# A hybrid attention/SSD block on one core: products grouped by unit, decay off GpSimd, a later B-times-C step, and an output split by token tile

## The chip, the core and the metric

One NeuronCore of a Trainium2 chip runs the whole kernel. Its engines are TensorE (PE, with its weight loads shown apart as PEld), VectorE (DVE), ScalarE (ACT), GpSimd (POOL) and SyncE (SP), which issues most of the DMAs. The metric is the device time of one execution in microseconds. The time before the change is 2100.9 us, the median of three runs (2100.33 to 2101.01).

## The reference

The input is 256 tokens of width 2048, in f32. Two token mixers work on one normalised input and are merged by sigmoid gates; a gated MLP with a short convolution follows.

```python
h = rms_norm(x, norm_mix_pre)
q, k, v, z, xbc, dt, g_sb, g_ssd = split(h @ w_in)
o_sb = stick_breaking_attention(q, k, v)          # 16 heads x 128
xs, bm, cm = split(silu(causal_dwconv(xbc, ...)))  # width 4
dt = softplus(dt + dt_bias); a = -exp(a_log)
y = ssd_scan(xs, dt, a, bm, cm)                    # 64 heads x 64, 8 groups, state 128
y = rms_norm((y + xs * d_skip) * silu(z), ssd_norm)   # by group of 512
merged = sigmoid(g_sb) * (o_sb @ w_sb_proj) + sigmoid(g_ssd) * (y @ w_ssd_proj)
x = x + rms_norm(merged @ w_out, norm_mix_post)
h = rms_norm(x, norm_ffn_pre)
gate, val = split(causal_dwconv(h @ w_up, ...))    # width 3, 5632 each
x = x + rms_norm((gelu(gate) * val) @ w_down, norm_ffn_post)
```

In the scan, `decay` is exp of the differences of a running sum `cs`, and counts only where the later token is not before the earlier one.

## The kernel before

**Weights.** All weight matrices lie in one array of units of 128 x 1024 f32 (512 KB), in the order of their use. `load` brings a unit from memory on SP's queue, `prep` splits it: ACT casts the high part `whi` (fp32r, L63), DVE subtracts to get the low part `wlo` (L64). `unit()` hands out the next unit and prepares up to three units ahead; five raw and five split buffers rotate. Activations are stored split in the same way, high and low side by side, in chunks of 4 tiles (`a`, `h`, `o`, `m`, `y`, `f`).

**Two kinds of product.** A *feature product* leaves features on the partitions: the weight tile is loaded as stationary operand and the activations stream. `feat_tile` (L109) issues for each of 16 input tiles a high product of 512 columns (high weights by high and low activations, L112) and then a low product of 256 columns (low weights by high activations, L113), both into one PSUM bank. One unit serves 8 such pairs. `feat_mm` makes one output tile, `feat_mms` several at once. Features are made this way for dt, x, B and C of the SSD mixer, q and k, and both halves of the FFN: 169 output tiles, 2704 pairs. A *token product* (`tok_mm`, L136) leaves tokens on the partitions: activations are loaded, weights stream, with three products of 512 columns for each input tile and token tile (L145 to L147); the 256 tokens are two token tiles.

**Order.** PE runs its products in the order in which a scheduler places the program's instructions; where `manual_schedule` stands, the program's own order is kept for the engines named. The SSD stage is a loop over 8 groups: four x tiles, one B and one C tile (feature products), then z (token products, L432). The work of a group's scan, `ssd_work` (L323), is a generator that `pump` moves one step ahead: after every feature tile, and after every fourth input tile of a token product. Its steps are: transposes of x to `px`, with the products by dt (`xw`), by the skip factors (`xd`, in the buffer `xs`), the decay differences `mm` from the row broadcast `csb` (L338) and their masking on POOL (L339); B times C in `pcb` (L343), the exponential (L347) and their product; `po`, the part from the state of the first half (L353); the diagonal part `pd` for each token tile (L363); the norm; and the transposes `pt` to the chunk `y` (L385). `xw`, `xs`, `mm` and `csb` are slots of 8 KB a partition.

**Ends.** At the start, ten small products (L171) run while the first loads come; x is loaded in halves between halves of the first unit (L181, L182). At the end, the last 512 columns of `w_down` are made for both token tiles by turns (L706); then come the sums of squares (`add`), the product with the norm's gain (`gained`), the root (`last`, `newton`) for both tiles together, and nine outputs, each stored as soon as it is made, by turns from SP's and ACT's queues (L727).

Of the kernel before, what the change touches and what calls it, by code (L numbers as in the profile page):

```python
# [17 lines left out]
P = 128  # L18
# [11 lines left out]
C_N = KT + C_FB + 88  # L30

LNEXP = "natural_log_exp_and_others"
ACT_DVE = {mybir.EngineType.Activation, mybir.EngineType.DVE}
# [5 lines left out]
def block_kernel(ctx, tc, xT, xN, wts, vecs, rows, hvec, dskip, gain, out):  # L39
# [69 lines left out]
    def feat_tile(ps, hi, lo, c, act, k, last):  # L109

        w = slice(c * P, (c + 1) * P)
        nc.tensor.matmul(ps, hi[:, w], act[:, k % 4, :, :].rearrange("p s t -> p (s t)"), start=(k == 0), stop=last)  # L112
        nc.tensor.matmul(ps[:, :T], lo[:, w], act[:, k % 4, 0, :], start=False, stop=last, skip_group_check=True)  # L113

    def feat_mm(acts, name):
        ps = mm_bank(name)
        for k in range(KT):
            if k % 8 == 0:
                hi, lo = unit()
            feat_tile(ps, hi, lo, k % 8, acts[k // 4], k, k == KT - 1)  # L120
        return ps

    def feat_mms(acts, pss):

        for kc in range(4):
            for i, ps in enumerate(pss):
                if i % 2 == 0:
                    hi, lo = unit()
                for k in range(4):
                    feat_tile(ps, hi, lo, 4 * (i % 2) + k, acts[kc], 4 * kc + k, 4 * kc + k == KT - 1)  # L130

    def feat_sum(ps, dst):
        nc.scalar.copy(dst, ps[:, T:])
        nc.vector.tensor_tensor(dst, dst, ps[:, :T], op=ALU.add)

    def tok_mm(acts, nk, name):  # L136

        pss = [mm_bank(f"{name}_{t}") for t in range(2)]
        for k in range(nk):
            if k % 2 == 0:  # L140
                hi, lo = unit()
            w = slice(k % 2 * 512, k % 2 * 512 + 512)
            for t in range(2):
                ah, al = (acts[k // 4][:, k % 4, s, t * P:(t + 1) * P] for s in range(2))
                nc.tensor.matmul(pss[t], ah, hi[:, w], start=(k == 0), stop=False)  # L145
                nc.tensor.matmul(pss[t], ah, lo[:, w], start=False, stop=False)  # L146
                nc.tensor.matmul(pss[t], al, hi[:, w], start=False, stop=(k == nk - 1))  # L147
            if k % 4 == 3:
                pump()
        return pss  # L150
# [19 lines left out]
    for i in range(10):  # L170
        nc.tensor.matmul(wake[:, :P], ones, ones, start=True, stop=True)  # L171
# [35 lines left out]
    for t in range(2):  # L207
        nc.sync.dma_start(x_tok[t], xN[t * P:(t + 1) * P, :])


    dsk = const.tile([P, 64], F32, name="dsk")
    nc.gpsimd.dma_start(dsk, dskip.partition_broadcast(P))
# [110 lines left out]
    def ssd_work(g, xf, bf, cf, xs, csb):  # L323
        h8 = slice(8 * g, 8 * g + 8)
        sz, xd = xs[:, 0], xs[:, 1]
# [3 lines left out]
        for t in range(2):  # L329
            px = paux.tile([P, 512], F32, tag="aux", name=f"px{g}_{t}")  # L330
            for j in range(4):
                nc.tensor.transpose(px[:, j * P:(j + 1) * P], xf[j][:, t * P:(t + 1) * P], ident)
            nc.vector.tensor_tensor(v3(xw[:, t, :]), v3(px), bc_in(dt_tok[:, t, h8], 64), op=ALU.mult)
            nc.scalar.copy(xd[:, t, :], px)
            nc.gpsimd.tensor_tensor(v3(xd[:, t, :]), v3(xd[:, t, :]), bc_in(dsk[:, h8], 64), op=ALU.mult)
        nc.gpsimd.tensor_tensor(v3(xw[:, 2, :]), v3(xw[:, 0, :]), bc_in(dec0[:, h8], 64), op=ALU.mult)
        for t in range(2):
            nc.vector.tensor_tensor(mm[:, t, :, :], csb[:, :, t * P:(t + 1) * P], bc_in(cs_tok[:, t, h8], P), op=ALU.subtract)  # L338
            nc.gpsimd.affine_select(out=mm[:, t, :, :], in_=mm[:, t, :, :], pattern=[[0, 8], [1, P]], compare_op=ALU.is_ge,  # L339
                                    fill=-30000.0, base=0, channel_multiplier=-1)  # L340
# [3 lines left out]
        nc.tensor.matmul(pcb[:, 256:384], bf[:, P:T], cf[:, P:T], start=True, stop=True)  # L344
        nc.scalar.copy(xw[:, 3, 0:P], pcb[:, P:T])
        lnexp()
        nc.scalar.activation(mm, mm, AF.Exp)  # L347
        for t in range(2):
            cb = pcb[:, 256 * t:256 * t + P].unsqueeze(1).broadcast_to([P, 8, P])
            nc.vector.tensor_tensor(mm[:, t, :, :], mm[:, t, :, :], cb, op=ALU.mult)  # L350
# [7 lines left out]
        nc.gpsimd.tensor_tensor(xd[:, 1, :], xd[:, 1, :], off, op=ALU.add)  # L358
        yield
        for t in range(2):  # L360
            pd = paux.tile([P, 512], F32, tag="aux", name=f"pd{g}_{t}")
            for h in range(8):
                nc.tensor.matmul(pd[:, h * 64:h * 64 + 64], mm[:, t, h, :], xw[:, t, h * 64:h * 64 + 64], start=True, stop=True)  # L363
            nc.vector.tensor_tensor(xd[:, t, :], xd[:, t, :], pd, op=ALU.add)
            yield
# [40 lines left out]
    stats_x()  # L406
    for g in range(GROUPS):
        xf = []
# [19 lines left out]
        csb = slot(F32, [8, T], f"csb{g}")  # L428
        nc.gpsimd.dma_start(csb, cs_dram[8 * g:8 * g + 8, :].partition_broadcast(P))
        xs = slot(F32, [2, 2, 512], f"xs{g}")  # L430
        bg.append(ssd_work(g, xf, bcs[0], bcs[1], xs, csb))
# [13 lines left out]
    drain()  # L445
    work.close()
# [126 lines left out]
    class PostNorm:  # L573
# [14 lines left out]
        def last(self):  # L588
            nc.vector.scalar_tensor_tensor(self.v, self.ss[:, :, 3], 1.0 / 2048, self.v, op0=ALU.mult, op1=ALU.add)
            nc.scalar.activation(self.q, self.v, AF.Ln)  # L590
            nc.scalar.activation(self.r, self.q, AF.Exp, scale=-0.5)

        def newton(self):
            nc.vector.tensor_tensor(self.q, self.r, self.r, op=ALU.mult)
            nc.vector.scalar_tensor_tensor(self.q, self.q, -0.5, self.v, op0=ALU.mult, op1=ALU.mult)
            nc.vector.scalar_tensor_tensor(self.r, self.q, 1.5, self.r, op0=ALU.add, op1=ALU.mult)
# [106 lines left out]
    for n in range(4):  # L703
        gfo = tmp.tile([P, 512], F32, tag="gfo", name=f"gfo{n}")
        nc.gpsimd.dma_start(gfo, rows[2, blk(n)].partition_broadcast(P))
        ps = tok_mm(f_ch, FF_T, f"ps_fo{n}")  # L706
# [102 lines left out]
```

## Time and profile before

| | us |
|---|---|
| median of three runs | 2100.9 |
| the profiled execution, from outside | 2101.31 |
| its span, first to last instruction | 2099.6 |
| PE busy | 2072.1 |
| DVE busy | 1386.0 |
| ACT busy | 1156.9 |
| POOL busy | 152.3 |

The span is what the profile covers; the trace's times count from its start. The first tiles and the SSD groups fill the time to 524 us, the gate and the SSD projection follow to 788, attention with its gate to 1171, two projections and the norm to 1357, the FFN's up products to 1847, and w_down to 2087. A row of the trace's timeline has start, duration, engine, line, operation, what is written and read, and shape; in brackets stands how long the engine was idle before it and who ended that. Matmuls overlap, so the distance from start to start is what one costs.

### The profile page before, as it was taken

Reading aid. Unit: us, or ns where it says so; the run is one execution under the profiler, and the core shown is the slowest. Engines: PE = TensorE matmul, PEld = TensorE weight load, DVE = VectorE, ACT = ScalarE, POOL = GpSimd, SP = SyncE. Lnnn points to the kernel's source line nnn. Section 1 sums busy time; section 2 is a strip of 40 time slices with the busy share of each in tenths; the row PEclk is TensorE's granted clock in tenths of the full one; section 3 lists DMA queues with packets and bytes.
Section 4 is the critical chain, followed back from the end, with each engine's and each line's share of the span. In section 5 each row is a group of like instructions: output and inputs, shape, how many; then the busy total and the mean of one; then the engine's idle time right before and its main releaser. Section 6 shows DMA issues by size and latency. Waiting matters only on the chain.

```text
span 2099.6 us, 27950 instructions
## 1 busy us (share of the span) xinstructions
PE 2072.1 (99%) x10632; PEld 1760.7 (84%) x10632; DVE 1386.0 (66%) x1794; ACT 1156.9 (55%) x1542; POOL 152.3 (7%) x134
## 2 busy tenths in 40 slices
PE   9999999999999999999999999999999999999997
PEld 7788888888888888888888888788888888888886
DVE  6888877788544445555544566598878887854443
ACT  6767677667543334555556444475555555544442
POOL 0222102222000000000000021100000000000000
PEclk9999999999999999999999999999999999999999
DMA  8564565555555555555555746475555555565653
GB/s 297 194 205 160 190 205 186 176 199 179 187 197 192 192 194 186 180 171 171 170 172 185 274 161 210 141 250 191 189 190 190 189 189 190 191 232 202 195 193 109
DMA packets 109094, 402.79 MB, mean 192 GB/s; under 512 B 12416, under 2 KB 12672, under 8 KB 106656
## 3 DMA queue, kind: packets, MB, share of 16 engines
q1 hardware_dynamic: 104912, 380.07, 54.1%
q0 software_dynamic: 3328, 20.02, 2.7%
q8 instruction: 83, 1.36, 0.3%
q10 hardware_dynamic: 720, 0.93, 0.1%
q14 instruction: 51, 0.42, 0.1%
HBM read 396.71 MB, written 4.26 MB: 191 GB/s over the span
## 4 chain that ended last, share of the span: by engine, by line
PE 92%; POOL 2%; DVE 2%; issue 2%; DMA 1%; ACT 1%; SPq 0%; DVEq 0%; ACTq 0%; POOLq 0%
PE ps_fv L112 8%; PE ps_fg L112 8%; PE ps_qk L112 6%; PE ps_xs L112 5%; PE ps_fo L147 4%; PE ps_fo L145 4%; PE ps_fo L146 4%; PE ps_fg L113 4%; PE ps_fv L113 4%; PE ps_qk L113 3%; PE ps_ssd L147 3%; PE ps_ssd L145 3%; PE ps_ssd L146 3%; PE ps_xs L113 2%; PE ps_bc L112 2%; PE ps_z L146 2%
## 5 line engine op out<-in xcount | busy, mean ns | idle before, releaser
L64 DVE TENSOR_TENSOR wlo<-raw,whi 128x1024 fp32r<-128x1024 f32 (+1 forms) x715 | 905.1, 1270 | 601.2 <-ACT whi L63 600.6
L63 ACT CAST whi<-raw 128x1024 fp32r<-128x1024 f32 (+1 forms) x715 | 746.2, 1051 | 793.7 <-PE ps_fo L147 128.9
L112 PE MATMUL ps_fg<-h,whi 128*128 128x512 f32 x688 | 240.7, 394 | 0.0
L112 PE MATMUL ps_fv<-h,whi 128*128 128x512 f32 x688 | 240.6, 394 | 0.0
L113 PE MATMUL ps_fg<-h,wlo 128*128 128x256 f32 x688 | 190.6, 277 | 0.0
L113 PE MATMUL ps_fv<-h,wlo 128*128 128x256 f32 x688 | 190.6, 277 | 0.0
L112 PE MATMUL ps_qk<-a,whi 128*128 128x512 f32 x512 | 181.3, 398 | 0.0
L112 PE MATMUL ps_xs<-a,whi 128*128 128x512 f32 x464 | 162.9, 396 | 0.0
L112 PEld LDWEIGHTS ps_fv<-h,whi 128*128 128x128 f32 x688 | 129.0, 188 | 30.0
L112 PEld LDWEIGHTS ps_fg<-h,whi 128*128 128x128 f32 x688 | 129.0, 188 | 30.0
L113 PE MATMUL ps_qk<-a,wlo 128*128 128x256 f32 x512 | 143.5, 280 | 0.0
L145 PE MATMUL ps_fo<-whi,f 128*128 128x512 f32 x352 | 136.9, 389 | 0.0
L147 PE MATMUL ps_fo<-whi,f 128*128 128x512 f32 x352 | 136.9, 389 | 0.0
L146 PE MATMUL ps_fo<-wlo,f 128*128 128x512 f32 x352 | 136.9, 389 | 0.0
L113 PEld LDWEIGHTS ps_fg<-h,wlo 128*128 128x128 f32 x688 | 129.2, 188 | 0.0
L113 PEld LDWEIGHTS ps_fv<-h,wlo 128*128 128x128 f32 x688 | 129.2, 188 | 0.0
L113 PE MATMUL ps_xs<-a,wlo 128*128 128x256 f32 x464 | 129.0, 278 | 0.0
L112 PEld LDWEIGHTS ps_qk<-a,whi 128*128 128x128 f32 x512 | 96.1, 188 | 22.6
L145 PE MATMUL ps_z<-whi,a 128*128 128x512 f32 x256 | 103.7, 407 | 0.0
L112 PEld LDWEIGHTS ps_xs<-a,whi 128*128 128x128 f32 x464 | 87.1, 188 | 19.6
L146 PE MATMUL ps_z<-wlo,a 128*128 128x512 f32 x256 | 100.4, 392 | 1.0 <-DVE wlo L64 1.0
L147 PE MATMUL ps_z<-whi,a 128*128 128x512 f32 x256 | 100.1, 391 | 0.0
(282 smaller groups left out, 3832.5 us busy)
## 6 DMA issues: line engine op xcount, KB each, us to landing
raw<-wts SPq DMA_DIRECT2D x713, 512.0 KB, 3.8
csb<-cs_dram POOLq DMA_DIRECT2D x8, 1024.0 KB, 8.1
xt<-xN SPq DMA_DIRECT2D x2, 1024.0 KB, 10.6
csb<-gain POOLq DMA_DIRECT2D x8, 256.0 KB, 4.1
xn<-xN POOLq DMA_DIRECT2D x2, 1024.0 KB, 7.9
x_dram<-xn POOLq DMA_DIRECT2D x2, 1024.0 KB, 9.0
xe<-x_dram POOLq DMA_DIRECT2D x2, 1024.0 KB, 10.3
x<-xT SPq DMA_DIRECT2D x3, 512.0 KB, 9.2
```

The source lines that it names most:

```text
L63: nc.scalar.copy(hi, src)
L64: nc.vector.tensor_tensor(lo, src, hi.bitcast(F32), op=ALU.subtract)
L112: nc.tensor.matmul(ps, hi[:, w], act[:, k % 4, :, :].rearrange("p s t -> p (s t)"), start=(k == 0), stop=last)
L113: nc.tensor.matmul(ps[:, :T], lo[:, w], act[:, k % 4, 0, :], start=False, stop=last, skip_group_check=True)
L145: nc.tensor.matmul(pss[t], ah, hi[:, w], start=(k == 0), stop=False)
L146: nc.tensor.matmul(pss[t], ah, lo[:, w], start=False, stop=False)
L147: nc.tensor.matmul(pss[t], al, hi[:, w], start=False, stop=(k == nk - 1))
```

## The change

- **Feature products by unit.** `feat_run` issues the high products of all 8 tiles of a unit, then all low ones. In `feat_mm` the second unit goes the other way round, low first. `feat_mms` takes two banks together.
- **SSD work.** The select on GpSimd is replaced: the difference goes through Relu with sign -1 and Exp with sign -1 on ACT (so it is never above 1), and B times C is masked with `m_le` on DVE. The scaling by `dec0` and the addition of the off-diagonal part move from POOL to DVE, and so does the product with the skip factors, read from PSUM. Multiplying the decay with B times C becomes a step of its own, so `po` comes one step later, and `pd` and `pt` too. From group 1 to the end of the gate PE keeps the program's order.
- **Skip factors** are columns of the vector load; their own DMA on POOL's queue goes.
- **Start.** Twelve instead of ten small products; the first quarter of x in one load, ahead of the first unit.
- **Tail.** For the last 512 columns the last 6 input tiles are done for token tile 0 first, then for tile 1 (`tok_mm_lag`), and everything behind runs tile by tile.

```diff
-    def feat_tile(ps, hi, lo, c, act, k, last):
-        w = slice(c * P, (c + 1) * P)
-        nc.tensor.matmul(ps, hi[:, w], act[:, k % 4, :, :].rearrange("p s t -> p (s t)"), start=(k == 0), stop=last)
-        nc.tensor.matmul(ps[:, :T], lo[:, w], act[:, k % 4, 0, :], start=False, stop=last, skip_group_check=True)
+    def feat_run(tiles, acts, hi_first):
+        for high in (hi_first, not hi_first):
+            for ps, hi, lo, k in tiles:
+                a, end = acts[k // 4][:, k % 4, :, :], k == KT - 1 and high != hi_first
+                if high:
+                    nc.tensor.matmul(ps, hi, a.rearrange("p s t -> p (s t)"), start=(k == 0), stop=end, skip_group_check=True)
+                else:
+                    nc.tensor.matmul(ps[:, :T], lo, a[:, 0, :], start=False, stop=end, skip_group_check=True)
...
     def feat_mm(acts, name):
         ps = mm_bank(name)
-        for k in range(KT):
-            if k % 8 == 0:
-                hi, lo = unit()
-            feat_tile(ps, hi, lo, k % 8, acts[k // 4], k, k == KT - 1)
+        for u in range(2):
+            feat_run(w_tiles(range(8 * u, 8 * u + 8), [ps]), acts, u == 0)
...
+    def tok_mm_lag(acts, nk, name, lag=3):
+        pss = [mm_bank(f"{name}_{t}") for t in range(2)]
+        held = []
+        for k in range(nk):
+            left = (nk - 1 - k) // 2
+            if k % 2 == 0:
+                w = unit(min(WBUFS - 2, left) if left < lag else WBUFS - 2)
+            if left < lag:
+                held.append((k, w))
+                tok_step(pss, acts, k, nk, 0, *w)
+            else:
+                for t in range(2):
+                    tok_step(pss, acts, k, nk, t, *w)
+        for k, w in held:
+            tok_step(pss, acts, k, nk, 1, *w)
+        return pss
...
-    for i in range(10):
+    for i in range(12):
...
+    nc.sync.dma_start(x_raw[0], xT[:, 0:4, :])
     for i in range(2):
-        nc.sync.dma_start(x_raw[0][:, 2 * i:2 * i + 2, :], xT[:, 2 * i:2 * i + 2, :])
         nc.sync.dma_start(raw0[:, i * 512:i * 512 + 512], wts[0][:, i * 512:i * 512 + 512])
...
             nc.vector.tensor_tensor(v3(xw[:, t, :]), v3(px), bc_in(dt_tok[:, t, h8], 64), op=ALU.mult)
-            nc.scalar.copy(xd[:, t, :], px)
-            nc.gpsimd.tensor_tensor(v3(xd[:, t, :]), v3(xd[:, t, :]), bc_in(dsk[:, h8], 64), op=ALU.mult)
-        nc.gpsimd.tensor_tensor(v3(xw[:, 2, :]), v3(xw[:, 0, :]), bc_in(dec0[:, h8], 64), op=ALU.mult)
-        for t in range(2):
-            nc.vector.tensor_tensor(mm[:, t, :, :], csb[:, :, t * P:(t + 1) * P], bc_in(cs_tok[:, t, h8], P), op=ALU.subtract)
-            nc.gpsimd.affine_select(out=mm[:, t, :, :], in_=mm[:, t, :, :], pattern=[[0, 8], [1, P]], compare_op=ALU.is_ge,
-                                    fill=-30000.0, base=0, channel_multiplier=-1)
+            nc.vector.tensor_tensor(v3(xd[:, t, :]), v3(px), bc_in(dsk[:, h8], 64), op=ALU.mult)
         yield
...
+        cbm = xw[:, 3, P:3 * P]
         nc.scalar.copy(xw[:, 3, 0:P], pcb[:, P:T])
+        for t in range(2):
+            nc.vector.tensor_tensor(cbm[:, t * P:(t + 1) * P], pcb[:, 256 * t:256 * t + P], m_le, op=ALU.mult)
         lnexp()
-        nc.scalar.activation(mm, mm, AF.Exp)
+        for t in range(2):
+            m = mm[:, t, :, :]
+            nc.vector.tensor_tensor(m, csb[:, :, t * P:(t + 1) * P], bc_in(cs_tok[:, t, h8], P), op=ALU.subtract)
+            nc.scalar.activation(m, m, AF.Relu, scale=-1.0)
+            nc.scalar.activation(m, m, AF.Exp, scale=-1.0)
+        nc.vector.tensor_tensor(v3(xw[:, 2, :]), v3(xw[:, 0, :]), bc_in(dec0[:, h8], 64), op=ALU.mult)
+        yield
...
-        nc.gpsimd.tensor_tensor(xd[:, 1, :], xd[:, 1, :], off, op=ALU.add)
+        nc.vector.tensor_tensor(xd[:, 1, :], xd[:, 1, :], off, op=ALU.add)
...
     with tc.manual_schedule(engines=ACT_DVE):
-        n3.add(3, 0, ps[0])
-        n3.add(3, 1, ps[1])
-        gained(3, 0, gfo)
-        n3.last()
-        gained(3, 1, gfo)
-        n3.newton()
-        for n in range(4):
-            for t in range(2):
+        for t in range(2):
+            w = slice(t, t + 1)
+            n3.add(3, t, ps[t])
+            gained(3, t, gfo)
+            n3.last(w)
+            n3.newton(w)
+            for n in range(4):
```

How the instructions stand on the engines shows where the steps went. First PE before, in z of group 3 (`ps_z3_0` and `ps_z3_1` are its two token tiles, the second number in a name is a buffer):

```order
L145 MATMUL ps_z3_1_2380<-whi79_2446,a2_153 128x512
L146 MATMUL ps_z3_1_2380<-wlo79_2447,a2_153 128x512
L147 MATMUL ps_z3_1_2380<-whi79_2446,a2_153 128x512
L353 MATMUL po3_2524<-xw3_2417 128x512
L145 MATMUL ps_z3_0_2379<-whi80_2464,a3_172 128x512
L146 MATMUL ps_z3_0_2379<-wlo80_2465,a3_172 128x512
L147 MATMUL ps_z3_0_2379<-whi80_2464,a3_172 128x512
```

and at the end of the same z, where the first x tile of group 4 (`ps_xs4_0`) follows:

```order
L145 MATMUL ps_z3_1_2380<-whi81_2490,a3_172 128x512
L146 MATMUL ps_z3_1_2380<-wlo81_2491,a3_172 128x512
L147 MATMUL ps_z3_1_2380<-whi81_2490,a3_172 128x512
L363 MATMUL pd3_0_2565<-xw3_2417,mm3_2418 128x64 x8
L112 MATMUL ps_xs4_0_2578<-a0_117,whi82_2508 128x512
L113 MATMUL ps_xs4_0_2578<-a0_117,wlo82_2509 128x256
```

PE now, at the end of z of group 3 and through that x tile:

```order
L148 MATMUL ps_z3_1_2372<-wlo81_2478,a3_173 128x512
L149 MATMUL ps_z3_1_2372<-whi81_2477,a3_173 128x512
L389 MATMUL po3_2549<-xw3_2409 128x512
L118 MATMUL ps_xs4_0_2557<-a0_118,whi82_2495 128x512 x4
L118 MATMUL ps_xs4_0_2557<-a1_137,whi82_2495 128x512 x4
L120 MATMUL ps_xs4_0_2557<-a0_118,wlo82_2496 128x256 x4
L120 MATMUL ps_xs4_0_2557<-a1_137,wlo82_2496 128x256 x4
L120 MATMUL ps_xs4_0_2557<-a2_154,wlo83_2516 128x256 x4
L120 MATMUL ps_xs4_0_2557<-a3_173,wlo83_2516 128x256 x4
L118 MATMUL ps_xs4_0_2557<-a2_154,whi83_2515 128x512 x4
L118 MATMUL ps_xs4_0_2557<-a3_173,whi83_2515 128x512 x4
L401 MATMUL pd3_0_2612<-xw3_2409,mm3_2410 128x64 x8
```

`po3` has moved from the middle of z to its end, and `pd3_0` from the end of z behind the first x tile; the x tile's products come as 8 high, 16 low and 8 high ones instead of by turns.

POOL before, from the row load of group 3 to that of group 4:

```order
L429 DMA csb3_2376<-cs_dram_225 128x2048
L336 TENSOR_TENSOR xw3_2417<-xw3_2417,dec0_223 128x512
L335 TENSOR_TENSOR xs3_2378<-xs3_2378,dsk_201 128x512 x2
L339 AFFINE_SELECT mm3_2418<-mm3_2418 128x1024 x2
L356 DMA csb3_2376<-gain 128x512
L358 TENSOR_TENSOR xs3_2378<-xs3_2378,csb3_2376 128x512
L429 DMA csb4_2955<-cs_dram_225 128x2048
```

and now, from group 2 to group 4:

```order
L355 DMA csb2_1793<-cs_dram_224 128x2048
L392 DMA csb2_1793<-gain 128x512
L355 DMA csb3_2369<-cs_dram_224 128x2048
L392 DMA csb3_2369<-gain 128x512
L355 DMA csb4_2945<-cs_dram_224 128x2048
```

Only the two loads of a group are left on that queue.

ACT before, from its last cast on (`n3_j` are squares, `n3_q` and `n3_r` the root):

```order
L63 CAST whi713_17594<-raw713_17592 128x1024
L571 ACTIVATE n3_j30_17648,n3_ss_16039<-ps_fo3_0_17266 128x512
L571 ACTIVATE n3_j31_17650,n3_ss_16039<-ps_fo3_1_17267 128x512
L590 ACTIVATE n3_q_16042<-n3_v_16040 128x2
L591 ACTIVATE n3_r_16041<-n3_q_16042 128x2
L727 DMA out_dram<-fo0_16037 128x512
L727 DMA out_dram<-fo1_16038 128x512
L727 DMA out_dram<-fo0_16037 128x512
L727 DMA out_dram<-fo1_16038 128x256
```

and now:

```order
L65 CAST whi713_17572<-raw713_17570 128x1024
L613 ACTIVATE n3_j30_17626,n3_ss_16017<-ps_fo3_0_17244 128x512
L633 ACTIVATE n3_q_16020<-n3_v_16018 128x1
L634 ACTIVATE n3_r_16019<-n3_q_16020 128x1
L770 DMA out_dram<-fo0_16015 128x512 x2
L613 ACTIVATE n3_j31_17643,n3_ss_16017<-ps_fo3_1_17245 128x512
L633 ACTIVATE n3_q_16020<-n3_v_16018 128x1
L634 ACTIVATE n3_r_16019<-n3_q_16020 128x1
L770 DMA out_dram<-fo1_16016 128x512
L770 DMA out_dram<-fo1_16016 128x256
```

Tile 0's root and two of its stores stand ahead of tile 1's squares (`n3_j31`) in ACT's queue now.

More of the change, by code (lines that the diff above doesn't have):

```diff
@@ L38, in block_kernel @@
 @with_exitstack
-def block_kernel(ctx, tc, xT, xN, wts, vecs, rows, hvec, dskip, gain, out):
+def block_kernel(ctx, tc, xT, xN, wts, vecs, rows, hvec, gain, out):
     nc = tc.nc
@@ L125, in feat_mms @@
         for kc in range(4):
[L126 to L130, printed above, removed]
+            for i in range(0, len(pss), 2):
+                feat_run(w_tiles(range(4 * kc, 4 * kc + 4), pss[i:i + 2]), acts, True)
     def feat_sum(ps, dst):
@@ L134, in feat_sum, with tok_step @@
         nc.vector.tensor_tensor(dst, dst, ps[:, :T], op=ALU.add)
+    def tok_step(pss, acts, k, nk, t, hi, lo):
+        w = slice(k % 2 * 512, k % 2 * 512 + 512)
+        ah, al = (acts[k // 4][:, k % 4, s, t * P:(t + 1) * P] for s in range(2))
+        nc.tensor.matmul(pss[t], ah, hi[:, w], start=(k == 0), stop=False)
+        nc.tensor.matmul(pss[t], ah, lo[:, w], start=False, stop=False)
+        nc.tensor.matmul(pss[t], al, hi[:, w], start=False, stop=(k == nk - 1))
     def tok_mm(acts, nk, name):
@@ L141, in tok_mm @@
                 hi, lo = unit()
[L142 removed]
             for t in range(2):
[L144 to L147, printed above, removed]
+                tok_step(pss, acts, k, nk, t, hi, lo)
             if k % 4 == 3:
                 pump()
+        return pss
[14 more added lines that the diff above has]
+            tok_step(pss, acts, k, nk, 1, *w)
         return pss
@@ L406, in block_kernel @@
     stats_x()
+    order = work.enter_context(ExitStack())
     for g in range(GROUPS):
+        if g == 1:
+            order.enter_context(tc.manual_schedule(engines=PE))
         xf = []
@@ L445, in block_kernel @@
     drain()
+    order.close()
     work.close()
```

51 lines of the change are left out of this document (32 added, 19 removed).

## The prediction

> **What bounds the kernel now.** I read the page's busy times first, then its chain that ended last, then who TensorE (PE) waits for, then the stretches in which one kind of product runs alone.
>
> ```profile
> span 2099.6 us, 27950 instructions
> PE 2072.1 (99%) x10632; PEld 1760.7 (84%) x10632; DVE 1386.0 (66%) x1794; ACT 1156.9 (55%) x1542; POOL 152.3 (7%) x134
> PE 92%; POOL 2%; DVE 2%; issue 2%; DMA 1%; ACT 1%; SPq 0%; DVEq 0%; ACTq 0%; POOLq 0%
> PE po L353 <- ACT xw L345: 3.7, 6, 0.7
> PE pth L385 <- DVE mog L632: 2.9, 1, 2.9
> PE ps_first L112 <- DVE a L197: 2.9, 2, 2.1
> PE po L353 <- POOL xw L336: 2.4, 1, 2.4
> ```
>
> PE is busy for 2072.1 of 2099.6 us and carries 92% of the chain. So there are only two ways to gain: PE's few waits (the last four rows: total, times, longest) with the ends of the kernel, or the pace of the products themselves. The wait rows name one thing that the change touches in the middle: the product `po` of the SSD work, 3.7 + 2.4 = 6.1 us. A busy PE is not proof of full pace, so I read that from stretches (us, then busy time and count by engine; the granted clock stands before the DMA share).
>
> ```profile
> 1400.00:1840.00 440.00, 440.00 (x2540) 384.79 (x2539) 355.34 (x558) 252.84 (x399) 0.00 (x0) 1.00 0.58 191
> 560.00:780.00 220.00, 220.00 (x972) 182.19 (x971) 102.81 (x87) 89.14 (x87) 0.00 (x0) 1.00 0.57 194
> 789.00:833.00 44.00, 44.00 (x251) 38.15 (x250) 25.09 (x31) 18.11 (x23) 0.00 (x0) 1.00 0.58 191
> ```
>
> The first is the FFN with feature products alone, a high one of 512 columns and a low one of 256 by turns: 440 us / 1270 pairs = 346.5 ns a pair. The second has token products of 512 columns alone: 220 / 972 = 226.3 ns each. The third is the attention's q and k, the same pairs as in the FFN, at 44 / 125.5 = 350.6 ns. What would they take by columns alone? At half the granted clock (a stretch quoted below) a pair's 768 columns go in 11.39 - 10.75 = 0.64 us:
>
> ```profile
> 10.75 0.63 PE L112 MATMUL ps_first<-a,whi 128*128 128x512 f32 x1
> 11.18 0.41 PE L113 MATMUL ps_first<-a,wlo 128*128 128x256 f32 x1
> 11.39 0.63 PE L112 MATMUL ps_first<-a,whi 128*128 128x512 f32 x1
> ```
>
> At full clock that is 320 ns a pair and 213.3 for 512 columns. So a token product has 226.3 - 213.3 = 13 ns on top, and an FFN pair 346.5 - 320 = 26.5, twice 13. Alternating high and low costs nothing in the FFN: the 13 ns go with each product, whatever stands beside it.
>
> **The change, part by part, against the profiled execution** (2101.3 us outside, span 2099.6; the median of the three runs, 2100.9, is 0.4 lower).
>
> *Grouped high and low products* (169 feature tiles of 16 pairs: 2704 pairs). Nothing is added or removed; only neighbours change. A high product behind a high one should take what a token product takes, 227 ns. A low one behind a low one is not in the trace in long runs; the nearest place is attention, where two products of 256 columns follow each other:
>
> ```profile
> 873.50 0.40 PE L500 MATMUL za<-sr,ntri_r 128*128 128x512 f32 x1
> 873.74 0.28 PE L501 MATMUL zb<-sr,ntri_r 128*128 128x256 f32 x1
> 873.86 0.28 PE L502 MATMUL za<-sr,nones_r 128*128 128x256 f32 x1
> 873.98 0.40 PE L500 MATMUL za<-sr,ntri_r 128*128 128x512 f32 x1
> 271.07 1.89 PE L363 MATMUL pd<-xw,mm 128*128 128x64 f32 x16
> 272.77 0.48 PE L112 MATMUL ps_xs<-a,whi 128*128 128x512 f32 x1
> ```
>
> Both start 120 ns after each other. With 227 that gives 347 a pair, as now. Bounds: the 64-column products of `pd`, each with its own weight load, come every (272.77 - 271.07) / 16 = 106 ns, so loads alone do not allow less than that: 14 ns less for a low product, -38 us in all if every low one went so fast. Above, the three of attention take 480 ns against 227 + 2 x 120 = 467 by the constant, so up to 13 ns too many; as 6.7 on each low product that is +18 us. I take 120, the row that is nearest, because it is the same width and number format.
>
> The Trainium skill ("TensorE: Matmul & The Clock Gate", Part 2, on LDWEIGHTS) puts a load of 128 columns at about 107 ns; the trace agrees with that pace (106), although it records 188 ns for a load. That speaks against the change as far as it goes: a low product of 120 leaves 13 ns for the next load, where a high one left over 100. By that page the run of low products still just fits, and the sum stays.
>
> What remains is the slower pattern of q and k. 512 pairs x (350.6 - 346.5) = 2.1 us there, and 0.9 us by my estimate in the first tiles and parts of the SSD stage (some 200 pairs with the same difference): -3.0 if all run as in the FFN. Against it stands a dearer high product behind a low one, once in 16 pairs, 169 times: by the attention rows (240 against 227) 13 ns, +1 to +2. **Together -2 us (from -38 to +18).**
>
> *SSD work.* What holds `po` back now:
>
> ```profile
> L338 DVE TENSOR_TENSOR mm<-csb,cs_tok x16: 1219/1730/2064, 80.3 to 506.8; 128x1024 f32<-128x1024 f32 x16
> 258.29 4.11 POOL L339 TENSOR_SCALAR_AFFINE_SELECT mm<-mm 128x1024 f32<-128x1024 f32 x2
> 262.43 1.92 ACT L347 ACTIVATE mm<-mm 128x2048 f32<-128x2048 f32 x1 [4.85 <-POOL mm L339]
> 264.25 0.24 ACT L345 COPY xw<-pcb 128x128 f32<-128x128 f32 x1
> 264.64 1.10 PE L353 MATMUL po<-xw 128*128 128x512 f32 x2 [0.61 <-ACT xw L345]
> ```
>
> GpSimd (POOL) selects for 4.1 us, ScalarE (ACT) waits 4.85 us for it, and the small copy that `po` needs stands behind the exponential in ACT's queue. The change takes the selects away (a Relu on ACT and a masked B times C do their work), scales with `dec0` on VectorE (DVE), and moves `po` one step of 4 k later: 24 products x 226.3 = 5.4 us. The longest of the six waits was 0.7, that of the first group 2.4, so both causes go, with room: **-6.1 us (-6.1 to 0)**. Late next on that path would be the copy behind Relu on ACT, which waits for DVE's subtraction; it now has over 5 us more.
>
> What is added has to fit beside PE:
>
> ```profile
> 253.00:316.00 63.00, 62.39 (x344) 53.45 (x343) 51.33 (x70) 44.91 (x61) 12.22 (x8) 1.00 0.57 188
> L333 DVE TENSOR_TENSOR xw<-px,dt_tok 128x512 f32<-128x512 f32 x3 | 2.0, 683 | 0.0
> ```
>
> DVE is busy 51.3 of the 63 us of a group. It gets two skip products from PSUM (683 each, as L333), the `dec0` scaling and the addition of the off-diagonal part (about as much each), and two masks of 128 columns (estimate 0.25 each): +3.2. The subtraction L338 takes 1219 at best, 1730 in the middle, while POOL works; without POOL that returns about 1.0. DVE comes to about 53.5, ACT (two copies less, a Relu about as long as the exponential's 1.92 more) stays under 47. Both stay under 63, weights are split three units ahead (3 x 8 pairs x 346.5 = 8.3 us), and PE never waits for them in these groups: 0. If that cover were gone, a late split would cost at most its own length, 1.4 us, once or twice a group; that is in the third rival. The queue of POOL now holds DMA issues alone (the row and gain loads), so nothing stands before them; the removed load of the skip factors on POOL, and the 64 more columns in the vector load on SP, move 32 KB at the start: 0.
>
> *Tail.* Today:
>
> ```profile
> 2085.81 0.39 PE L147 MATMUL ps_fo<-whi,f 128*128 128x512 f32 x1
> 2086.24 0.60 ACT L571 ACTIVATE n_j<-ps_fo 128x512 f32<-128x512 f32 x1 [11.87 <-PE ps_fo L147]
> 2086.49 0.39 PE L147 MATMUL ps_fo<-whi,f 128*128 128x512 f32 x1
> 2086.95 0.69 DVE L701 TENSOR_TENSOR fo<-ps_fo,gfo 128x512 f32<-128x512 f32 x1 [11.33 <-ACT n_j L571]
> 2087.63 0.16 DVE L589 SCALAR_TENSOR_TENSOR n_v<-n_ss,n_v 128x2 f32<-128x2 f32 x1
> 2087.83 0.20 ACT L590 ACTIVATE n_q<-n_v 128x2 f32<-128x2 f32 x1 [0.23 <-DVE n_v L589]
> 2088.89 5.52 DVE L726 SCALAR_TENSOR_TENSOR fo<-fo,n_r,xe 128x512 f32<-128x512 f32 x9
> 2089.68 4.71 ACTq L727 DMA_DIRECT2D out_dram<-fo  x4
> 2094.05 0.34 ACTq L727 DMA_DIRECT2D out_dram<-fo  x1
> ```
>
> Token tile 0 is ready 18 products, 4.1 us, before tile 1 after the change. Its last product starts at 2086.49 - 4.07 = 2082.42 instead of 2085.81, 3.4 earlier. With the rows' own distances its squares start at 2082.84, the first of its four outputs at 2085.49, and the fourth ends at 2088.15 (seven whole and two half outputs take 5.52 now, so about 0.66 and 0.45 each). But ACT issues two of tile 0's stores ahead of tile 1's squares in its queue, and the second store waits for the third output, 2087.47; with 0.34 for the issue, tile 1's squares run from about 2087.9 instead of 2086.9. From there: gain product at 2088.6, its sum of squares and root as in the rows (1.94 from gain product to first output), outputs from 2090.55, three whole and two half ones in 2.9 us: 2093.4, against 2088.89 + 5.52 = 2094.41. **-1.0 us**; without the wait behind the store it would be -2, and if the stores at the end run no sooner than now, 0.
>
> *Start.*
>
> ```profile
> 8.69:15.52 6.83, 5.57 (x17) 4.80 (x18) 5.11 (x9) 5.86 (x10) 0.00 (x0) 0.50 1.03 415
> ```
>
> PE runs at half clock from 8.69 to 15.52, after it waited for the second half of the first x load; its 5.57 busy us would have been 2.8. Two more wake products, x in one load and four high products before the next data may or may not keep the clock up. The data come at the same pace, so I take 0 (-2.8, or +1.7 if another half of such a stretch came on top). The Trainium skill (same page, Part 1) says that the gate looks at free-running windows of 3.4 us and releases after a busy one: the 6.83 us are two such windows. By it, a fuller second window would give the 2.8 back.
>
> Sum: -2 - 6.1 - 1.0 + 0 = -9.1, from 2101.3 to 2092.2; less the 0.4 by which the median lies below the profiled run: **2091.8 us**.
>
> **Rivals.**
> 1. *Slower: the run of low products is paced by weight loads.* Each low product leaves PE only 120 ns to take in the next weights, sixteen times in a row, where now a 230 ns product stands between. At 126.7 ns, the size of the 13 ns too many in attention, 2704 x 6.7 = +18.1, less the 3.0 that q and k could regain, less 7.1 from the rest: 2101.3 + 8.0 = 2109. It decides from 120 + (7.1 + 3.0) / 2704 = 123.7 ns a low product. For it: alternation hides each load best. Against it: `pd` takes loads at 106.
> 2. *Low products faster than 120.* At 112 to 117 in a run: 2704 x 3 to 8 = -8 to -22, so 2070 to 2084. For it: in the FFN the next high product starts 110 to 120 ns after a low one. Against it: the pair sums to 346 all the same, and what the low one saves there the high one takes.
>
> ```profile
> 1400.36 0.27 PE L113 MATMUL ps_fv<-h,wlo 128*128 128x256 f32 x1
> 1400.47 0.40 PE L112 MATMUL ps_fv<-h,whi 128*128 128x512 f32 x1
> ```
> 3. *The SSD wait only changes its name:* PE waits for DVE or ACT at `po`, `pd` or `pt` as long as before, since DVE now holds all that POOL did. Then 2101.3 - 3.0 - 0.4 = 2097.9. Against it: the slack of 5.4 us. For it: ACT and DVE take their queues in order, and Relu waits in front of the copy.
>
> **How the numbers follow.** A measurement of this kernel can tell about 0.2%, 4.2 us. The forecast (2087 to 2096) has 0.62; rival 1 0.12, rival 2 0.13, rival 3 0.13. Leaving out rival 1 and the lower part of rival 2 (0.09) gives the range 2083 to 2099. Faster by over 0.2% means under 2096.7: forecast and rival 2, 0.75. Within: rival 3, 0.13. Slower (over 2105.1): rival 1, 0.12.
>
> **What would show it.** In the FFN stretch the mean pair decides the first part: 346.5 ns right, 353 rival 1, under 343 rival 2. Wait rows for `po` should be gone and none above 0.5 us for `pd` or `pt` in their place. From the last product to the last output should take about 6.9 instead of 7.9 us. The stretch at half clock near 10 us tells the start. The prediction is wrong in kind if the time changes while FFN pairs and waits do not.

## The result, and the profile after the change

| | before | after |
|---|---|---|
| median, us | 2100.95 (4 runs, 2100.33 to 2101.60) | 2090.18 (4 runs, 2089.61 to 2090.45) |
| profiled execution, from outside | 2101.31 | 2089.61 |
| its span | 2099.6 | 2087.9 |

The ratio is 0.9946, with a 95% interval of 0.9934 to 0.9958: about 11 us faster, where 9 were forecast. The page of the changed kernel begins:

```profile
span 2087.9 us, 27925 instructions
PE 2069.3 (99%) x10636; PEld 1767.5 (85%) x10636; DVE 1376.5 (66%) x1846; ACT 1164.4 (56%) x1547; POOL 64.9 (3%) x85
```

PE is as full as before, and only 2.8 us of its busy time went. So I read where each stage's first product starts in the two timelines, and took differences (one execution of each kernel):

| stretch | before, us | after, us | difference |
|---|---|---|---|
| start to the first z product | 51.6 | 49.0 | -2.6 |
| rest of the SSD stage and its gate | 562.5 | 554.8 | -7.7 |
| SSD projection | 174.1 | 174.1 | 0 |
| q, k, v and attention | 288.7 | 287.1 | -1.6 |
| attention's gate to the norm | 280.0 | 280.0 | 0 |
| FFN up products | 490.4 | 492.7 | +2.3 |
| w_down, to the last product's start | 239.2 | 239.1 | 0 |
| last product to last output | 7.9 | 6.8 | -1.1 |
| last output to the end of the span | 5.2 | 4.1 | -1.1 |

They sum to the 11.7 us between the spans. Whom PE waits for after the change, four of seven rows (total, times, longest); the first, `pth`, transposes the merged result at the norm and waits 2.9 us before the change too:

```profile
PE pth L423 <- DVE mog L676: 3.1, 2, 2.9
PE rx_ps L281 <- DVE rx_dg L280: 1.7, 1, 1.7
PE ps_first L118 <- DVE a L226: 1.2, 2, 0.8
PE pt L423 <- DVE xs L412: 0.3, 1, 0.3
```

The two rows of `po` are gone, and no row of `pd` came. A wait of 1.0 us for a weight split in group 0's z went too. New is `rx_ps`, the spreading of the first norm over the partitions: PE is ready there 4.5 us earlier than before (35.59 against 40.11), and the second half of DVE's part starts only 2.4 us earlier (36.96 against 39.35). The start itself, as a stretch (PE's busy time first, clock ahead of the DMA share) and as rows:

```profile
8.69:15.52 6.83, 6.83 (x42) 6.04 (x41) 6.20 (x10) 6.41 (x12) 0.00 (x0) 1.00 1.03 413
```

```profile
5.08 0.91 ACT L225 ACTIVATE a<-x,gpre 128x256 fp32r<-128x256 f32 x2 [2.55 <-DMA gpre<-vecs]
6.41 0.91 ACT L225 ACTIVATE a<-x,gpre 128x256 fp32r<-128x256 f32 x2
7.67 1.81 PE L118 MATMUL ps_first<-a,whi 128*128 128x512 f32 x6 [0.39 <-DVE a L226]
```

The clock is full from 8.69 to 15.52, where it was half before. ACT takes the second half of x at 6.41 instead of 8.87, and PE waits 0.39 us instead of 2.13. The FFN, first as a stretch of 440 us, then as runs of equal products:

```profile
1390.00:1830.00 440.00, 440.00 (x2532) 388.93 (x2531) 350.75 (x557) 260.21 (x397) 0.00 (x0) 1.00 0.59 190
```

```profile
1399.83 2.08 PE L120 MATMUL ps_fv<-h,wlo 128*128 128x256 f32 x16
1401.74 2.00 PE L118 MATMUL ps_fv<-h,whi 128*128 128x512 f32 x8
1403.58 1.98 PE L118 MATMUL ps_fg<-h,whi 128*128 128x512 f32 x8
1405.39 2.08 PE L120 MATMUL ps_fg<-h,wlo 128*128 128x256 f32 x16
1407.31 2.00 PE L118 MATMUL ps_fg<-h,whi 128*128 128x512 f32 x8
1409.14 1.98 PE L118 MATMUL ps_fv<-h,whi 128*128 128x512 f32 x8
1410.96 2.08 PE L120 MATMUL ps_fv<-h,wlo 128*128 128x256 f32 x16
```

440 / 1266 = 347.6 ns a pair, against 346.5. From one run of equal products to the next: sixteen low ones take 1401.74 - 1399.83 = 1.91 us (119 each), sixteen high ones 1405.39 - 1401.74 = 3.65 (228 each). A tile takes (1410.96 - 1399.83) / 2 = 5.565 us; by turns it took 16 x 346.5 = 5.544. Last, the tail:

```profile
2076.91 0.39 PE L149 MATMUL ps_fo<-whi,f 128*128 128x512 f32 x1
2080.89 2.87 DVE L769 SCALAR_TENSOR_TENSOR fo<-fo,n_r,xe 128x512 f32<-128x512 f32 x5
```

### The profile page after: what moved, and what is told of

The parts are those of the page before. It is cut to its first block, busy times and chain, and to the rows that moved or that the text cites. A ratio compares the mean times of both kernels' runs of the same rounds, so it can differ in the third digit from the quotient of the medians.

```text
span 2087.9 us, 27925 instructions
## 1 busy us (share of the span) xinstructions
PE 2069.3 (99%) x10636; PEld 1767.5 (85%) x10636; DVE 1376.5 (66%) x1846; ACT 1164.4 (56%) x1547; POOL 64.9 (3%) x85
## 4 chain that ended last, share of the span: by engine, by line
PE 94%; DVE 3%; issue 1%; DMA 1%; ACT 1%; DVEq 0%; ACTq 0%
PE ps_fg L118 7%; PE ps_fv L118 7%; PE ps_qk L118 6%; PE ps_xs L118 4%; PE ps_fv L120 4%; PE ps_fg L120 4%; PE ps_fo L147 4%; PE ps_fo L148 4%; PE ps_fo L149 4%; PE ps_qk L120 3%; PE ps_ssd L147 3%; PE ps_ssd L148 3%; PE ps_ssd L149 3%; PE ps_z L148 3%; PE ps_z L147 3%; PE ps_z L149 3%
## 5 line engine op out<-in xcount | busy, mean ns | idle before, releaser
L66 DVE TENSOR_TENSOR wlo<-raw,whi 128x1024 fp32r<-128x1024 f32 (+1 forms) x715 | 885.5, 1240 | 494.9 <-ACT whi L65 489.5
L118 PE MATMUL ps_fg<-h,whi 128*128 128x512 f32 x688 | 171.3, 391 | 0.0
L118 PE MATMUL ps_fv<-h,whi 128*128 128x512 f32 x688 | 171.1, 391 | 0.0
L118 PE MATMUL ps_qk<-a,whi 128*128 128x512 f32 x512 | 125.9, 393 | 0.0
L118 PE MATMUL ps_xs<-a,whi 128*128 128x512 f32 x464 | 119.1, 401 | 0.0
L147 PE MATMUL ps_ssd<-whi,y 128*128 128x512 f32 x256 | 99.6, 389 | 0.0
L148 PE MATMUL ps_ssd<-wlo,y 128*128 128x512 f32 x256 | 99.6, 389 | 0.0
L149 PE MATMUL ps_ssd<-whi,y 128*128 128x512 f32 x256 | 99.6, 389 | 0.0
L120 PEld LDWEIGHTS ps_fg<-h,wlo 128*128 128x128 f32 x688 | 88.2, 191 | 3.4
L120 PEld LDWEIGHTS ps_fv<-h,wlo 128*128 128x128 f32 x688 | 88.2, 191 | 3.3
L120 PE MATMUL ps_fv<-h,wlo 128*128 128x256 f32 x688 | 89.2, 283 | 0.0
```

Of the source, the lines that this page charges most:

```text
L66: nc.vector.tensor_tensor(lo, src, hi.bitcast(F32), op=ALU.subtract)
L118: nc.tensor.matmul(ps, hi, a.rearrange("p s t -> p (s t)"), start=(k == 0), stop=end, skip_group_check=True)
L120: nc.tensor.matmul(ps[:, :T], lo, a[:, 0, :], start=False, stop=end, skip_group_check=True)
```

## Experiments

Each kernel is the changed one with one edit, except where the heading says otherwise. The number behind a kernel's name is its median in us. The kernel before ran beside them, at medians of 2101.4, 2102.1 and 2101.5 in three sittings.

**No step of its own for the decay (2089.22), and the selects back on GpSimd (2088.92).**

```diff
-        yield
         for t in range(2):
             cb = cbm[:, t * P:(t + 1) * P].unsqueeze(1).broadcast_to([P, 8, P])
```


> The changed kernel without the step of its own: decay times B-times-C in the step of the exponential, so po comes 24 products (5.4 us) earlier; GpSimd stays out. Theory A (the later step removed the waits): waits of po, or of another product of that work, of 0.3 to 0.8 us in each group, 2092 to 2096. Rival B (GpSimd's removal is enough): no waits, 2090.2.

```diff
-            nc.scalar.activation(m, m, AF.Relu, scale=-1.0)
-            nc.scalar.activation(m, m, AF.Exp, scale=-1.0)
+            nc.gpsimd.affine_select(out=m, in_=m, ..., fill=-30000.0, base=0, channel_multiplier=-1)
+            nc.scalar.activation(m, m, AF.Exp)
```


> The changed kernel with the selects on GpSimd put back between the difference and the exponential (Relu goes); the step of its own stays, so po has 24 products more. Theory A (the later step is what removed the waits of po): no wait of po again, 2090.2, within 0.5. Rival B (getting GpSimd out of the path did it): po waits about 0.7 us in each group, 2094 to 2096.

Four rows of PE's waits, without the step and then with the selects (`wake` are the small products at the start):

```profile
PE rx_ps L281 <- DVE rx_dg L280: 1.3, 1, 1.3
PE wake L200 <- DVE ones L197: 1.1, 1, 1.1
PE ps_first L118 <- DVE a L226: 1.0, 2, 0.6
PE ptm L422 <- DVE gat L593: 0.4, 1, 0.4
```

```profile
PE rx_ps L281 <- DVE rx_dg L280: 1.7, 1, 1.7
PE wake L200 <- DVE ones L197: 1.1, 1, 1.1
PE ps_first L118 <- DVE a L226: 1.0, 2, 0.6
PE pt L424 <- DVE xs L413: 0.6, 1, 0.6
```

Neither waits at `po`, nor at `pd`. So neither edit is needed where the other stands, with the products grouped: theory A holds for the second kernel and rival B for the first. (In the second only the selects are back; GpSimd's other work stays on DVE.) The ratios, 0.9939 in both (0.9926 to 0.9951, and 0.9925 to 0.9952), cannot be told from the change's own 0.9946.

**The kernel before, with grouping alone (2097.6; ratio 0.9985, 0.9976 to 0.9994).** Its edit is the part of the change's diff around `feat_run`.

> The kernel before with feature products grouped by unit, and nothing else of the change. Theory A (grouping costs 20 ns a feature tile, and its gain is only that no execution and no stage falls into the pattern of 353 ns a pair): FFN tiles 5567 ns (+1.8 to +2.3 us), q and k -1.6, SSD stage +0.9 to +1.3, waits of po stay, 2101 + 1.7 = 2102.7 (2099.5 if the start wait of before goes too), and no execution about 8 us above the rest. Rival B (grouping is part of the gain of an ordinary execution): 2099 or less with the start as before.

Faster by 3.9 us by the medians of this sitting (2101.47 and 2097.6), as rival B said: 2099 or less with the start as before. By stages (profiled execution, 2097.33 against 2101.31): the SSD stage from its first z product -3.2, q, k and attention -1.6, FFN +1.5, start -0.3, the rest -0.4. PE's waits here:

```profile
PE ps_first L116 <- DVE a L203: 3.0, 1, 3.0
PE po L359 <- POOL xw L342: 2.4, 1, 2.4
PE po L359 <- ACT xw L351: 0.2, 1, 0.2
```

Of the 3.7 us at `po` behind ACT 0.2 is left, although GpSimd still selects and no step was added. The rows of one group show how, before and then grouped:

```profile
255.37 2.06 DVE L338 TENSOR_TENSOR mm<-csb,cs_tok 128x1024 f32<-128x1024 f32 x1
257.75 0.59 PE L343 MATMUL pcb<-bc,bc 128*128 128x256 f32 x2
```

```profile
253.09 2.06 DVE L344 TENSOR_TENSOR mm<-csb,cs_tok 128x1024 f32<-128x1024 f32 x1
255.96 0.59 PE L349 MATMUL pcb<-bc,bc 128*128 128x256 f32 x2
261.97 0.24 ACT L351 COPY xw<-pcb 128x128 f32<-128x128 f32 x1
```

From DVE's subtraction to ACT's copy both take 8.88 us (before: 264.25 - 255.37; grouped: 261.97 - 253.09). But DVE begins 2.38 us ahead of PE's `pcb` before, and 2.87 ahead when grouped. In all six groups that waited 0.6 us the lead grows so, from 2.3 or 2.4 to 2.8 or 2.9, and 0.1 to 0.2 is left of the wait. The group that had a lead of 2.89 before waited only 0.1 then too. Why DVE is further ahead was not tried.

**Products by turns again, everywhere (median 2093.62 of 12) and in the FFN alone (2090.11 of 8).**

```diff
-        for high in (hi_first, not hi_first):
-            for ps, hi, lo, k in tiles:
...
+        order = [(t, high) for t in tiles for high in (True, False)]
+        for (ps, hi, lo, k), high in order:
...
```


> The changed kernel with high and low feature products by turns again, everywhere. Theory A (grouping costs a little, because a run of low products is paid back by the first high products behind it: about 21 ns a feature tile in the FFN): the 88 FFN tiles return to 16 x 346.7 = 5547 ns each, -2.1 us by ps_fo; q and k fall back to the slower pattern (mean pair above 350), +1.6; the SSD stage -1.3; the start stays at full clock, so 2090.2 - 1.8 = 2088.4. Rival B (the four and eight high products at the start are what keeps the clock up): the start has a stretch at half clock again, +2.6, about 2091.0. Rival C (grouping brought part of the gain): above 2092.

> The changed kernel with products by turns in the FFN alone, grouped elsewhere. Theory A: FFN tiles 5547 ns instead of 5567 or more, nothing else moves, 2090.2 - 2.2 = 2088.0. Rival (the FFN's 2.1 us come from something else, such as later weights): no change, 2090.

The executions fall into two groups. Everywhere: seven from 2090.46 to 2093.83 and five from 2098.66 to 2101.45. FFN alone: six from 2087.05 to 2090.44 and two at 2097.6 and 2098.67. The profiled executions are one of each, at 2098.66 and 2090.27. Their FFN stretches, everywhere and then FFN alone:

```profile
1390.00:1830.00 440.00, 440.00 (x2492) 381.66 (x2492) 347.82 (x546) 246.94 (x391) 0.00 (x0) 1.00 0.58 187
```

```profile
1390.00:1830.00 440.00, 440.00 (x2540) 387.94 (x2539) 354.98 (x558) 252.49 (x398) 0.00 (x0) 1.00 0.59 190
```

One runs at 440 / 1246 = 353.1 ns a pair, the other at 346.5, at the same clock and with no wait between products. So products by turns have two paces. The slow one repeats every three pairs (113, 233, 117, 241, 120 and 236 ns from start to start), and is the one that q and k had before the change. In the FFN it is worth about 9 us: 499.6 us in the first of these executions, 490.5 in the second. At the good pace the FFN gives back 2.2 us against grouping, as expected; the 2.7 us that this execution had lost by q and k hide it. No other execution of the six has a trace, and their median, 2089.7, does not show the 2.2 either. That start had the changed kernel's code, but x came later: the first feature product at 7.31 instead of 6.55, 3.4 us at half clock, and longer waits for group 0's work. Of the 47 executions of the kernel before in these runs two took 2107.5 and 2107.7, the rest 2099.5 to 2103.3. Whether these two had the slow pace is not shown: they have no trace, and their mean clock is 0.993, where the others show 0.994 to 0.997. By that difference some 4 to 6 of their 6 us would be lost clock (an estimate: 0.0025 of 2106 us, the clock being rounded). All 60 executions of the grouped kernels, each among its own, lie within 2.8 us.

The kernel with turns everywhere also shows the SSD edits without grouping. Two rows of PE's waits there, of eight:

```profile
PE rx_ps L282 <- DVE rx_dg L281: 1.6, 1, 1.6
PE ps_z L149 <- DVE wlo L66: 1.0, 1, 1.0
```

No row names `po`, and from the first z product to the SSD projection this kernel takes 555.4 us, against 562.5 before and 554.8 after. So these edits earn 7.1 us alone, where grouping alone earns 3.2. Together they earn 7.7 and not the sum, since both remove the same waits behind ACT.

**High products first in both units of a tile (2091.84).** Runs of low products are half as long, and twice as many.

```diff
-            feat_run(w_tiles(range(8 * u, 8 * u + 8), [ps]), acts, u == 0)
+            feat_run(w_tiles(range(8 * u, 8 * u + 8), [ps]), acts, True)
```


> The changed kernel with the high products first in both units of a tile: twice as many runs of low products, half as long (8 instead of 16). Theory A (the price is one of each run of low products, paid by the high ones behind it): FFN tiles 5587 instead of 5567 ns, 169 x 20 ns = +3.4 us, 2093.5. Theory B (the price goes by the number of low products): tiles stay at 5567, 2090.2. Theory C (the price goes faster than the length of the run): tiles under 5567, below 2089.

```profile
1404.01 2.00 PE L118 MATMUL ps_fg<-h,whi 128*128 128x512 f32 x8
1409.60 2.00 PE L118 MATMUL ps_fv<-h,whi 128*128 128x512 f32 x8
```

A tile takes 5.59 us, 0.02 more than with one run: the price is one for each run of low products. From start to start in the FFN of the changed kernel, the first low product behind a high one takes 113 ns and all others 119 to 120; the first five high ones behind the run take 233, 236, 228, 233 and 231, the next ones 227. Five times a few nanoseconds, less the first 7, make some 20 ns. The kernel lost 1.7 us where +3.4 was expected: +1.8 in the FFN and +0.5 in q and k, as the price says, but nothing in the SSD stage.

**The start: x in halves (2090.29), ten wake products (2089.89), and the whole start as before (2092.91).**

```diff
+    dsk = const.tile([P, 64], F32, name="dsk")
+    nc.gpsimd.dma_start(dsk, dskip.partition_broadcast(P))
...
-    nc.sync.dma_start(x_raw[0], xT[:, 0:4, :])
     for i in range(2):
+        nc.sync.dma_start(x_raw[0][:, 2 * i:2 * i + 2, :], xT[:, 2 * i:2 * i + 2, :])
...
-    for i in range(12):
+    for i in range(10):
```


> The changed kernel with the first quarter of x in halves between the halves of the first weight unit, as before; twelve wake products and grouping stay. Theory A (one load of x removes TensorE's 2.1 us wait for the second half, and with it the half clock): the wait of about 2 us and a stretch at half clock near 10 us come back, the first z product starts near 51.3 instead of 48.7, time about 2092.8. Rival B (the clock is kept by grouping or by the two wake products): wait back, clock stays full, first z product near 49 to 50, since the later wait of 1.7 us at rx_ps takes up the difference; 2090 to 2091.

> The changed kernel with ten instead of twelve wake products. Theory A (the load of x matters, the wake products do not): first products and clock as in the changed kernel, 2090.2. Rival (the two products keep the clock up): half clock from 8 to 15 us, about 2.6 us more, 2092.8.

> The changed kernel with its whole start as before: x in halves, ten wake products, and the skip factors by a DMA of their own on GpSimd's queue. Since halves alone and ten wake products alone left the clock full and no wait for x, two theories are left. Theory A (the skip factors' DMA at the start delays the second half of x): that half lands near 8.9 us, TensorE waits about 2 us for it, and the stretch from 8.69 to 15.52 runs at half clock; the first z product near 51 and 2092 to 2093 in all. Rival B (the wait of before's profiled execution was a hazard of that execution): x lands by 6 us, clock full, 2089.5 to 2090.5.

The stretch of the start with halves, with ten wake products, and with the whole start as before:

```profile
8.69:15.52 6.83, 6.83 (x42) 6.03 (x41) 5.82 (x9) 6.37 (x12) 0.00 (x0) 1.00 1.02 412
```

```profile
8.69:15.52 6.83, 6.83 (x36) 5.86 (x36) 6.43 (x12) 6.35 (x12) 0.00 (x0) 1.00 1.03 414
```

```profile
8.69:15.52 6.83, 6.38 (x28) 5.47 (x29) 5.84 (x10) 5.82 (x10) 0.00 (x0) 0.75 1.03 416
```

The timeline with halves alone, and with the whole start as before:

```profile
5.72 0.91 ACT L225 ACTIVATE a<-x,gpre 128x256 fp32r<-128x256 f32 x2
```

```profile
1.32 0.69 POOL L239 DMA_DIRECT2D dsk<-dskip  x1 [0.80 <-POOLq L847]
8.06 0.91 ACT L225 ACTIVATE a<-x,gpre 128x256 fp32r<-128x256 f32 x2 [2.39 <-DMA x<-xT]
9.14 1.22 PE L118 MATMUL ps_first<-a,whi 128*128 128x512 f32 x2 [2.68 <-DVE a L226]
```

Halves alone and ten of the small products that wake PE at the start change nothing, each by itself. With the skip factors' load back as well, issued by GpSimd at 1.32 us, the second half of x comes at 8.06 instead of 5.72 (halves alone), PE waits 2.68 us, and the clock is half for 3.4 us. That costs 2.7 us in all, as theory A said. Neither the load with x in one piece nor halves with ten wake products but without the load was tried, so that the load needs one of them is not excluded. The load goes with a hole in the transfers. This is the microsecond from 5 to 6, before, with the whole start as before, and in the changed kernel (the last two numbers are DMA share and GB/s):

```profile
5.00:6.00 1.00, 0.59 (x4) 0.40 (x3) 0.58 (x2) 1.00 (x3) 0.00 (x0) 1.00 0.55 102
5.00:6.00 1.00, 0.91 (x5) 0.72 (x5) 0.98 (x3) 0.68 (x2) 0.00 (x0) 1.00 0.46 64
5.00:6.00 1.00, 0.75 (x7) 0.56 (x6) 0.38 (x1) 0.92 (x3) 0.00 (x0) 1.00 0.95 293
```

The three traces with the load move 51 to 102 GB/s in that microsecond, and the eleven without it 244 to 399. ACT takes the second half of x at 8.06 to 8.87 in the three, and at 5.72 to 7.17 in the eleven. Why 32 KB should make the hole is not shown. Nor is the clock safe without the load: in the traced execution with turns in the FFN alone, where x came at 7.17, it was half for 3.4 us.

**The tail as before (2091.37).**

```diff
-        ps = (tok_mm if n < 3 else tok_mm_lag)(f_ch, FF_T, f"ps_fo{n}")
+        ps = tok_mm(f_ch, FF_T, f"ps_fo{n}")
...
-        for t in range(2):
-            w = slice(t, t + 1)
-            n3.add(3, t, ps[t])
-            gained(3, t, gfo)
-            n3.last(w)
-            n3.newton(w)
+        n3.add(3, 0, ps[0])
+        n3.add(3, 1, ps[1])
...
```


> The changed kernel with the tail as before (both token tiles by turns, roots and outputs together). Theory A: from the last product's start to the last output 7.9 instead of 6.8 us, and from there to the end of the span about 1.1 more, since the stores of both tiles land together: 2090.2 + 2.2 = 2092.4. Rival (only the output moves, the stores do not): 2091.3.

```profile
span 2089.1 us, 27917 instructions
```

```profile
2076.14 0.39 PE L149 MATMUL ps_fo<-whi,f 128*128 128x512 f32 x1
2078.54 5.52 DVE L770 SCALAR_TENSOR_TENSOR fo<-fo,n_r,xe 128x512 f32<-128x512 f32 x9
```

The first row is the page's, the others the timeline's. From the last product to the last output 2084.06 - 2076.14 = 7.92 us, and 5.0 more to the end: 12.96 against 10.99 with the new tail. The tail is worth 2.0 us, half of it behind the last output, where only one tile's stores are still landing. The median says 1.2, near the rival's 2091.3. The traced execution stood 0.8 us ahead at the SSD projection, which hides as much of the tail's worth; the others have no trace.

**PE's order in the SSD groups left to the scheduler (2090.59).**

```diff
-            order.enter_context(tc.manual_schedule(engines=PE))
+            pass
```


> The changed kernel with TensorE's order in the SSD groups left to the scheduler. Theory A (the place of the steps in the program is enough): 2090.2, within 0.5, no new waits. Rival (the scheduler places po or pd ahead of their inputs, as before): waits of 0.5 us or more in the groups, 2092 to 2096.

The scheduler gives the same order: all 10636 products in the trace follow each other as in the changed kernel. This part of the change does nothing, and the run is a measure of chance. Its profiled execution took 2091.68 against 2089.61, and it stands 2.4 us behind at the first product of the SSD stage's gate already (at group 0's `pt` alone it waits 1.7 instead of 0.3).

**Towards a faster one: no step, and the norm's diagonal ahead of a weight split (2089.30).**

```diff
     stats_x()
+    rx_dg = diag(rstd_tok, "rx")
```


> The changed kernel without the step of its own for decay times B-times-C, and with the diagonal for the first norm's broadcast made on VectorE right behind that norm's root, ahead of a weight split of 1.2 us. Theory A (what is left at the start is TensorE's wait at rx_ps for VectorE): that wait falls from 1.3 or 1.7 to 0.1 to 0.5 us, and the time to about 1 us under the kernel without the step: 2088.2. Rival (the wait comes back as a late weight split, or in group 0): no gain, 2089.2.

```profile
PE ps_first L118 <- DVE a L226: 1.9, 2, 1.5
PE ps_z L148 <- DVE wlo L66: 1.1, 1, 1.1
```

The wait at `rx_ps` is gone, and PE waits 1.1 us for a weight split behind it. In this trace the other order on DVE only moves the wait. The kernel is no faster than without the step alone.

## Why the prediction was right, and where it was not

- **Sum.** 2091.8 was forecast and 2090.18 came. In the profiled execution the start gave 2.6 us where 0 was forecast, the tail 2.2 where 1.0 was, the SSD stage 7.7 where 6.1 was for `po`, and the FFN cost 2.3 where about 1 was. That the sum came so near is in part luck.
- **Pace of grouped products.** Right in kind: low ones cost 119 to 120 ns, high ones 227 to 228, and an FFN pair is 347.6. Rival 1 (loads as pace, 126.7) and rival 2 (112 to 117) fall. The term for mixed neighbours was too small: I put 13 ns on one high product behind a low run, and there are five dearer ones, some 20 ns a tile in all, or 1.8 us in the FFN's 88 tiles. The FFN lost 2.3 us in the profiled execution, and 1.5 to 3.1 in ten traces with one run of low products a tile.
- **q and k.** -1.6 measured, -2.1 and some 0.4 back forecast. I took the 350.6 ns for a property of that stage; it is a second pace of products by turns, which took the FFN too in a kernel with the rest of the change. Grouped, no trace shows it, and the 60 executions stay within 2.8 us of each other, each among its own. Whether the kernel before ever lost these 9 us in its FFN is not shown: its trace has the good pace there.
- **`po`.** The waits went as forecast, 6.1 us; the stage gained 7.7, where 1.0 more is the wait for a weight split. With products grouped, each of the later step and GpSimd's removal is enough; grouping alone removes most of the wait behind ACT, and the SSD edits alone remove all. The step "both causes go, with room" gave a right size and told nothing of which edit earns it. Rival 3 falls: its own wait rows did not come.
- **Start.** This is the step that failed: "The data come at the same pace, so I take 0", and "the removed load of the skip factors on POOL [...]: 0". The second half of x came 2.5 us earlier. Put back with x in halves and ten wake products, the load costs the whole 2.6 us again (first z product at 51.6 instead of 49.0). I looked for the gain in the wake products and the load of x, which do nothing by themselves. The gain lies within the bounds that the forecast gave for the start, -2.8 to +1.7. The Trainium skill's rule on the clock ("TensorE: Matmul & The Clock Gate", Part 1: free-running windows of 3.4 us) agrees with the traces: at the start, half clock for 6.8 us before, 3.4 with the start undone, none after.
- **Tail.** The last output came 6.8 us behind the last product (6.9 forecast). The 1.1 us from there to the end of the span were not in the sum, which followed the last output and not its stores.

## What to carry to other kernels

When a wait has several causes in a chain, removing any one can be enough, so undo each edit alone before paying for all of them. Before calling a stage slower than another, look for two paces of the same code, and run it often enough to see both. Before tuning the first products, look at what the DMA queues move in the first microseconds: here a start with one small load more on another queue was 2.7 us longer.

## What the runs showed of the hardware that I had not expected

- High and low fp32r products by turns ran at one of two paces, 346.5 or 353.1 ns a pair, at full clock and without waits. What decides between them stays open.
- A run of 8 or of 16 products of 256 columns, each with its own weights, cost about 20 ns in all: 26 on the five products of 512 columns behind it, less 7 on its own first.
- A 32 KB broadcast load issued by GpSimd at 1.3 us went with a hole in the transfers (51 to 102 GB/s from 5 to 6 us, against 244 to 399 without it) and with the second half of the first x load, on SP's queue, coming 2.3 us later (8.06 against 5.72).
